# Input projections by seven products of quarters, ahead of the heads, in a two-branch decoder step

## The chip, the cores and the metric

The kernel runs on one core of one Trainium2 chip. The metric is device time in microseconds, from start to end of the program. TensorE (PE) multiplies, VectorE (DVE) and GpSimd (POOL) work on elements, ScalarE (ACT) evaluates functions and copies, and SyncE (SP) issues the transfers. Each engine takes its instructions in its own written order and waits on semaphores of the others.

## The reference

One decoder layer on 560 tokens (16 meta, 512 prompt, 32 sample tokens: 8 batches of 4), width 1024, float32. The core of it:

```python
hn = rmsnorm(x, norm_g)
proj = jnp.einsum('btd,dn->btn', hn, w_in)          # 1024 -> 14344 columns
a_pool, z_pool, q, k, v, o, z_m, i_pre, f_pre, g_pool, g_mlstm = split_projection(proj)
y_pool = multiscale_pool(pool_buf, a_pool, pos0, w_pool, pool_scale) * jax.nn.silu(z_pool)
...
state, h = mlstm_scan(qh, kh, vh, ig, lf, (C, n, m), n_lead)   # 4 heads of 512
h = ((h - mu) * lax.rsqrt(var + EPS)).reshape(B, T, MLSTM_WIDTH) * mh_norm_g
y_mlstm = jax.nn.sigmoid(o) * h * jax.nn.silu(z_m)
u = (jax.nn.sigmoid(g_pool) * (y_pool @ w_branch_pool)
     + jax.nn.sigmoid(g_mlstm) * (y_mlstm @ w_branch_mlstm))
x_out = x + u @ w_out                                # then a last rmsnorm
```

Each head has a 512 x 512 matrix memory C; the kernel returns the new ones for the prompt and for the 8 sample batches, besides the layer's output, the normalisers, stabilisers and pool rows.

## The kernel before, in words

Every float32 operand is held as a sum of two float32r tiles, hi and lo, and every product takes three matmuls: lo hi, hi lo, hi hi (`mm3`, line 129). `weights` (line 113) loads a block of 1024 x 128 weights in one transfer of 512 KB, makes hi on ScalarE (L108) and lo on VectorE (L111). A projection of 128 columns is 8 k blocks x 3 matmuls for each half of the tokens, 48 matmuls of 272 or 280 columns, with the 128 x 128 weights stationary and the normalised tokens `hT_hi`, `hT_lo` moving.

`begin` normalises and transposes the tokens and does the first two blocks of the pool branch; `gates` (line 338) computes everything that has one value per head and token, a chain of small instructions on VectorE. `pooling` projects the pool branch, mixes it, multiplies by its branch weights and stores `up_d`. Then four times `head(h)` (line 580): `unit_v` projects the values with tokens stationary and 512 columns moving (L607, L609); `unit_q`, `unit_k`, `unit_o`, `unit_z` project in blocks of 128; between them stand the head's own products: transposed keys (`k_rows`, L695), the prompt's memory (`prompt_C`, L709), the sample batches' (`sample_C`: read C, L726 and L732, update on VectorE L733, store), scores, key sums, denominators and numerators (L793, L795). The last step of a head, `variances` (line 864), is put into the next head's value projection: a product with ones, the square root on ScalarE (L870), a reciprocal on VectorE (L871), four multiplications. `final` has the merge gates, the mLSTM branch product, the output product and the last norm.

A scheduler with a timing model chooses the order of each engine's instructions among the program's steps; only `Pinned` steps of the beginning keep the written order. Tiles come from rings: `r` (29 tiles of 560 words, queries, keys and other rows), `c` (12 tiles of 1024 words, weights and C) and 8 banks of PSUM. SyncE issues all the large transfers in order.

Of the kernel before, what the change touches and what calls it, by code (L numbers as in the profile page):

```python
# [16 lines left out]
P = 128  # L17
# [14 lines left out]
# token columns: 16 meta, 512 prompt, 32 sample (batch-major)  # L32
# [7 lines left out]
HALF_ALL = ((0, 280), (280, 560))  # L40
HALF_OUT = ((16, 288), (288, 560))


def constants():
# [15 lines left out]
    # rows of the sample queries' part: batches b and b + 4 side by side  # L60
# [8 lines left out]
class Pinned:  # L69
    """An engine whose instructions keep the order they are written in."""  # L70
# [9 lines left out]

class Trunk:
    RS, CS = 29, 12
    G0, Y0 = 1, 3

    def __init__(self, tc, I, O):
        self.tc, self.nc, self.I, self.O = tc, tc.nc, I, O
        self.n = 0
        self.first = []

# [7 lines left out]
    # slabs shared by all phases: [P, 560] and [P, 1024] words  # L97
# [3 lines left out]
    def c(self, name, dt=F32, shape=(D,)):  # L101
        return self.mp.tile([P, *shape], dt, tag="c", name=self.name(name), bufs=self.CS)

    # a float32 tile as the exact sum of two float32r tiles
# [15 lines left out]
    def wcols(self, c0, c=P):  # L120
# [3 lines left out]
    def mm3(self, out, stats, movs):  # L124
        seq = []
        for (sh, sl), (mh, ml) in zip(stats, movs):
            seq += [(sl, mh), (sh, ml), (sh, mh)]
        for j, (s, m) in enumerate(seq):
            self.nc.tensor.matmul(out, s, m, start=(j == 0), stop=(j == len(seq) - 1))  # L129

    def project(self, w, mov, halves, m=P):
        return [self.project_half(w, mov, *t, m) for t in halves]

    def project_half(self, w, mov, t0, t1, m=P):
        hi, lo = w
        ps = self.ps()
        self.mm3(ps[:m, :t1 - t0],
                 [(hi[:, k, :m], lo[:, k, :m]) for k in range(hi.shape[1])],
                 [mov(k, t0, t1) for k in range(hi.shape[1])])
        return ps  # L140

    def hn(self, k, t0, t1):
        return self.hT[0][:, k, t0:t1], self.hT[1][:, k, t0:t1]
# [7 lines left out]
    def run(self):  # L151
        with ExitStack() as ctx:
            tc, nc, I = self.tc, self.nc, self.I
            self.mp = ctx.enter_context(tc.tile_pool(name="main", bufs=1))
            self.psum = ctx.enter_context(tc.tile_pool(name="psum", bufs=8, space=PSUM))
            self.dram = ctx.enter_context(tc.tile_pool(name="scratch", bufs=1, space=DRAM))
            self.w_in = I["w_in"][0].rearrange("(k p) n -> p k n", p=P)
            self.rows_d = self.dram.tile([H, ROWN], F32, name="rows_d")
            self.up_d = self.dram.tile([P, 8, NO], F32, name="up_d")
            self.y_d = self.dram.tile([P, 12, NO], F32, name="y_d")  # L160
            with tc.tile_pool(name="early", bufs=1) as self.ep:
                self.begin()
                self.pooling()
            with tc.tile_pool(name="heads", bufs=1) as self.hp:
                self.heads_begin()
                for h in range(H):
                    self.head(h)
                self.heads_end()
            with tc.tile_pool(name="final", bufs=1) as self.fp:
                self.final()  # L170

# [1 line left out]
    def x_rows(self, t, j):  # L173
        nc, I = self.nc, self.I
        if j == 0:
            nc.sync.dma_start(t[16:], I["x_prompt"][0, 0:112])
            nc.sync.dma_start(t[:16], I["meta_tokens"])
        elif j < 4:
            nc.sync.dma_start(t, I["x_prompt"][0, 128 * j - 16:128 * j + 112])
        else:  # L180
            nc.sync.dma_start(t[:16], I["x_prompt"][0, 496:512])
            nc.sync.dma_start(t[16:48], I["x_sample"].rearrange("b t d -> (b t) d"))

    def begin(self):
        nc, I, mp, ep = self.nc, self.I, self.mp, self.ep
        V, A, G = nc.vector, nc.scalar, nc.gpsimd
        xs = [self.c("x") for _ in range(5)]
        grow = self.c("grow")[:1]
# [8 lines left out]
        wraw = [self.c("wraw", shape=(NK, P)) for _ in range(2)]  # L197
        nc.sync.dma_start(wraw[0], self.wcols(CA))
        self.x_rows(xs[2], 2)
        nc.sync.dma_start(wraw[1], self.wcols(CA + P))  # L200
# [10 lines left out]
        self.hT = [mp.tile([P, NK, NT], F32R, tag="hT", name=n, bufs=2) for n in ("hT_hi", "hT_lo")]  # L211
        self.hS = mp.tile([P, NK, 112], F32R, name="hS")
# [5 lines left out]
        raw = ep.tile([P, NK, 64], F32, name="wg_raw")  # L218
# [3 lines left out]
        seg = ep.tile([H, 2, NT], F32, name="seg")  # L222
# [210 lines left out]
    def pooling(self):  # L433
# [97 lines left out]
        for g in range(1, 4):  # L531
# [3 lines left out]
            if g == 1:  # L535
                self.gate_columns(a)
# [546 lines left out]
```

## Time and profile before

| what | value |
|---|---|
| runs | 1130.87, 1136.81 and 6162.49 us; median 1136.81 |
| profiled execution: span on the core | 1129.6 us (its own time is not listed beside it) |
| mean granted TensorE clock | 0.997 of full speed |
| TensorE, VectorE, ScalarE, GpSimd busy | 1112.0, 613.9, 373.6, 218.8 us |
| matmuls | 7938 |
| transfers | 177.18 MB, mean 157 GB/s |

Busy times count instructions of an engine, overlaps once. A matmul's end is modelled: its duration reads 0.29 us where the next one starts 0.13 us later, so the price of a matmul is read from the spacing of starts in the timeline. In the list of groups a row is one kind of instruction with its count, its busy time and the mean of one in ns, then the idle time of the engine just ahead of it and what ended it.

### The profile page before, as it was taken

How to read it: one execution, taken by the hardware profiler on the slowest of the kernel's cores; microseconds unless marked ns; L12 is line 12 of the kernel's file. 1: busy time of each engine (PE TensorE's matmuls, PEld its weight loads, DVE VectorE, ACT ScalarE, POOL GpSimd, SP SyncE). 2: the span in 40 equal slices, each digit the busy share in tenths (PEclk: the TensorE clock that was granted, in tenths of full speed). 3: DMA queues.
4: the chain of work that ended last, by engine and by line, in shares of the span. 5: the costliest groups of instructions: out<-in, count | busy, mean ns of one | idle time of the engine just before them, and what ended most of it. 6: DMA issues, size and time to landing. Idle time of an engine off the chain costs nothing.

```text
span 1129.6 us, 19419 instructions
## 1 busy us (share of the span) xinstructions
PE 1112.0 (98%) x7938; PEld 1016.7 (90%) x7938; DVE 613.9 (54%) x954; ACT 373.6 (33%) x688; POOL 218.8 (19%) x367
## 2 busy tenths in 40 slices
PE   7999999999999999999999999999999989999997
PEld 6999999989879889979889979889978889999976
DVE  6786732224545755446655456556447465265633
ACT  5642342113222343232342232343222334342322
POOL 4223220003205003205003215003214001020000
PEclk9999999999999999999999999999999999999999
DMA  8432433434566744566654566754565754343512
GB/s 210 128 110 73 111 86 107 126 97 113 178 204 211 231 143 135 176 203 221 222 164 124 173 193 204 232 176 118 167 223 192 237 179 133 107 132 118 180 52 84
DMA packets 188176, 177.18 MB, mean 157 GB/s; under 512 B 12479, under 2 KB 137167, under 8 KB 187563
## 3 DMA queue, kind: packets, MB, share of 16 engines
q1 hardware_dynamic: 188087, 175.94, 50.9%
q8 instruction: 62, 1.02, 0.4%
q14 instruction: 27, 0.22, 0.1%
HBM read 127.80 MB, written 47.39 MB: 155 GB/s over the span
## 4 chain that ended last, share of the span: by engine, by line
PE 77%; DMA 9%; DVE 8%; issue 2%; ACT 1%; SPq 1%; POOL 0%; DVEq 0%; POOLq 0%; ACTq 0%
PE ps L129 57%; PE ps L607 8%; DMA wraw<-in_w_in_dram 6%; DVE C L733 3%; PE ps L709 3%; PE ps L726 2%; PE ps L795 1%; DMA out_dram<-C 1%; PE ps L609 1%; ACT whi L108 1%; DVE wlo L111 1%; DVE vc L767 1%; DMA x<-in_x_prompt_dram 1%; PE ps L695 1%; PE ps L732 1%
## 5 line engine op out<-in xcount | busy, mean ns | idle before, releaser
L129 PE MATMUL ps<-hT_hi,wlo 128*128 128x272 f32 (+1 forms) x1504 | 439.5, 292 | 0.3 <-DVE yp L493 0.3
L129 PE MATMUL ps<-hT_hi,whi 128*128 128x272 f32 (+1 forms) x1504 | 435.3, 289 | 0.0
L129 PE MATMUL ps<-hT_lo,whi 128*128 128x272 f32 (+1 forms) x1504 | 435.1, 289 | 0.0
L111 DVE TENSOR_TENSOR wlo<-wraw,whi 128x1024 fp32r<-128x1024 f32 x134 | 168.0, 1254 | 338.3 <-ACT whi L108 227.0
L129 PEld LDWEIGHTS ps<-hT_hi,wlo 128*128 128x128 f32 x1504 | 284.2, 189 | 15.1 <-issue 10.4
L129 PEld LDWEIGHTS ps<-hT_hi,whi 128*128 128x128 f32 x1504 | 284.7, 189 | 0.0
L129 PEld LDWEIGHTS ps<-hT_lo,whi 128*128 128x128 f32 x1504 | 283.8, 189 | 0.2
L108 ACT CAST whi<-wraw 128x1024 fp32r<-128x1024 f32 x134 | 140.6, 1049 | 393.7 <-DMA wraw<-in_w_in_dram 313.6
L733 DVE SCALAR_TENSOR_TENSOR C<-C,bc,ps 128x512 f32<-128x512 f32 x128 | 87.4, 739 | 6.6 <-PE ps L732 6.6
L129 PE MATMUL ps<-yh,whi 128*128 128x272 f32 x256 | 72.9, 288 | 0.0
L129 PE MATMUL ps<-yl,whi 128*128 128x272 f32 x256 | 72.8, 288 | 0.0
L129 PE MATMUL ps<-yh,wlo 128*128 128x272 f32 x256 | 70.5, 289 | 0.0
L111 POOL TENSOR_TENSOR vl<-v,vh 128x512 fp32r<-128x512 f32 x16 | 31.8, 2023 | 110.3 <-issue 84.5
L607 PE MATMUL ps<-whi,hT_lo 128*128 128x512 f32 x128 | 50.5, 395 | 0.0
L607 PE MATMUL ps<-whi,hT_hi 128*128 128x512 f32 x128 | 50.4, 393 | 0.0
L607 PE MATMUL ps<-wlo,hT_hi 128*128 128x512 f32 x128 | 50.2, 393 | 0.0
L129 PEld LDWEIGHTS ps<-yh,whi 128*128 128x128 f32 x256 | 48.2, 188 | 0.0
L129 PEld LDWEIGHTS ps<-yl,whi 128*128 128x128 f32 x256 | 48.2, 188 | 0.0
L129 PEld LDWEIGHTS ps<-yh,wlo 128*128 128x128 f32 x256 | 46.9, 188 | 0.0
L726 PE MATMUL ps<-C,qm 128*32 128x512 f32 x256 | 40.7, 603 | 0.0
L111 POOL TENSOR_TENSOR kl<-k,kh 128x560 fp32r<-128x560 f32 x16 | 22.3, 1396 | 90.2 <-DVE r_hi L673 77.3
L129 PE MATMUL ps<-ypl,whi 128*128 128x272 f32 x128 | 36.9, 288 | 0.0
(315 smaller groups left out, 1806.7 us busy)
## 6 DMA issues: line engine op xcount, KB each, us to landing
wraw<-in_w_in_dram SPq DMA_DIRECT2D x112, 512.0 KB
C<-in_state_C_dram SPq DMA_DIRECT2D x64, 512.0 KB
out_dram<-C SPq DMA_DIRECT2D x64, 512.0 KB
wraw<-in_w_branch_mlstm_dram SPq DMA_DIRECT2D x16, 512.0 KB
bc<-rows_d SPq DMA_DIRECT2D x4, 1256.0 KB
wraw<-in_w_branch_pool_dram SPq DMA_DIRECT2D x8, 512.0 KB
out_dram<-c SPq DMA_DIRECT2D x16, 256.0 KB
wraw<-in_w_out_dram SPq DMA_DIRECT2D x8, 512.0 KB
```

What stands on the lines that cost most here:

```text
L108: nc.scalar.copy(hi, src)
L111: (lo_on or nc.gpsimd).tensor_tensor(lo, src, hi.bitcast(F32), ALU.subtract)
L129: self.nc.tensor.matmul(out, s, m, start=(j == 0), stop=(j == len(seq) - 1))
L607: nc.tensor.matmul(pv[i], s, w[:, k2], start=(k == 0 and j == 0), stop=(k == 7 and j == 2))
L609: nc.tensor.matmul(pv[4][:112], self.hS[:, k], w[:, k2], start=(k == 0 and j == 0), stop=(k == 7 and j == 1))
L695: nc.tensor.transpose(ps[:, i * P:(i + 1) * P], kw[:, i * P:(i + 1) * P], self.ident)
L709: nc.tensor.matmul(pc, s[:, i], m[:, i], start=(i == 0 and j == 0), stop=False)
L726: nc.tensor.matmul(pqc[r:r + 32], self.qm[:, d, 32 * b:32 * b + 32], Cs[bb // 2][:, bb % 2], start=(d == 0 and g == 0), stop=(d == 3 and g ...
L732: nc.tensor.matmul(pu, kwst[r:r + 12, g], vst[r:r + 12, g], start=True, stop=True, tile_position=(r, 0))
L733: V.scalar_tensor_tensor(C, C, wintb[:, b, 3:4], pu, ALU.mult, ALU.add)
L767: V.scalar_tensor_tensor(t[:n], vh[:n, i].bitcast(F32), vs[:n, i:i + 1], vl[:n, i].bitcast(F32), ALU.subtract, ALU.add)
L795: nc.tensor.matmul(pb[:, o:o + mv.shape[-1] - m], s, mv[:, m:], start=(j == 0), stop=(j == last[True]))
```

## The change

**The product by quarters.** `quad` takes a pair of blocks, 256 columns, at once. The weights are cut into quarters by the two halves of the 1024 inputs and the two blocks of 128 columns; the tokens into quarters by the same halves of the inputs and two halves of 280 tokens (the token columns are laid out anew for this, `COLS`, with `HN` = 280). Seven products of sums of quarters take the place of the eight products of quarters, each of 4 k blocks x 3 matmuls. Four sums of token quarters are made once (`quarter_sums`, on GpSimd, VectorE and ScalarE); four sums of weight quarters are made for each pair on VectorE. Partial results stay in PSUM across products or are kept by ScalarE (`keep`) and added by VectorE (`total`). 47 pairs go this way: q, k, o and z of the heads, z, the merge gates and three of four inputs of the pool branch. The values are projected as before.

**The order.** All projections now stand ahead of the heads, as a list of units. `weave` writes a unit's products side by side with the next unit's weight work, the last but one's late steps, and the steps on the sample's C. Results go to DRAM (`q_d`, `k_d`, `v_d`, `og_d`, `yp_d`, `sg_d`, `qc_d`) and come back in `attention`, where one head's products are woven with the next head's loads and splits. `final` multiplies the pool branch first, with the last head's `variances` in it, then the mLSTM branch, merges and projects.

**Rings.** The 1024-word ring becomes `raw` (4 tiles) and `hl` (14 tiles, seven for each pair); `r` has 12 tiles.

```diff
+def weave(*lists):
+    steps = sorted(((i + 0.5) / len(l), n, i) for n, l in enumerate(lists) for i in range(len(l)))
+    for _, n, i in steps:
+        lists[n][i]()
...
-    def weights(self, src, a, c):
-        raw = self.c("wraw", shape=(a, c))
-        self.nc.sync.dma_start(raw, src)
-        hi, lo = self.c("whi", F32R, (a, c)), self.c("wlo", F32R, (a, c))
-        self.split(hi, lo, raw, self.nc.scalar, self.nc.vector)
-        return hi, lo
...
+    def quad(self, src, lo, dst, scale=None, f21=None, after=(), then=()):
...
+        ahead = [hi1, lambda: hi("w2", "b"), low1, lambda: low("w2", "b"), lambda: add("a", 0, "a", 1),
+                 lambda: add("a", 1, "b", 1), lambda: add("b", 1, "a", 0), lambda: hi("wa", "a"),
+                 lambda: add("b", 0, "b", 1), lambda: hi("wb", "b"), lambda: low("wb", "b"), lambda: low("wa", "a")]
...
+        def p1():
+            product("A", [(w["1"][:, 0, k], w["1"][:, 1, k]) for k in range(4)], quarter(0, 0), True)
+            keep("A", "p1")
+        def p2():
+            product("X", cols("w2", 0), quarter(0, 1), True)
+            total("11", "X", "p1", 1, 1)
+        def p6():
+            product("A", cols("wb", 1), combined("b"), False)
+            keep("A", "u")
+        def p5():
+            product("E", cols("wa", 0), combined("a"), True)
+            keep("E", "e")
+        def p7():
+            product("A", cols("wa", 1), combined("c"), False)
+            total("22", "A", "e", -1, 1)
+        def p3():
+            product("E", cols("w2", 1), combined("d"), False)
+            total("12", "E", "u", 1, -1)
+        def p4():
+            product("A", cols("wb", 0), quarter(1, 1), False)
...
+        for t, u in enumerate(units):
+            if t + 2 < end:
+                for f in units[t + 2].load:
+                    f()
...
+            weave(u.products, units[t + 1].ahead if t + 1 < end else [], old.then + before.after, extra, done)
+            old, before = before, u
...
+        for h, u in enumerate(heads):
+            n = heads[h + 1] if h < 3 else Unit()
+            if h < 3:
+                weave(u.scores, n.ahead1)
+                weave(n.rows, heads[h - 1].late if h else [], n.ahead2[-1:], u.sums)
+            else:
+                weave(u.scores, heads[2].late)
+                weave(u.sums)
+            weave(u.numerators, n.ahead3 if h < 3 else [])
+        self.late = lambda: weave(heads[3].late)
```

Where the change moves instructions, three places matter. First VectorE's queue in the projections of head 0, before, at the first o and z blocks (`sz` is the gate of z, `wlo` the low part of a weight block, `vc` the centred values, C the sample's memory):

```order
L733 SCALAR_TENSOR_TENSOR C_3763<-C_3763,bc_2640,ps_3778 128x512
L836 TENSOR_TENSOR sz_3839<-ps_3789,sz_3839 128x272
L836 TENSOR_TENSOR sz_3839<-ps_3814,sz_3839 128x272
L837 SCALAR_TENSOR_TENSOR og_3603<-og_3603,gmh,sz_3839 128x544
L111 TENSOR_TENSOR wlo_4046<-wraw_4043,whi_4045 128x1024
L767 SCALAR_TENSOR_TENSOR vc_3884<-vh_2643,vs_2645,vl_2644 128x512
```

The same queue now, one pair of weights (`ra`, `rb`) from its first low part to its last, with the totals of the running pair (`zm`) and of the next (`so`) in between:

```order
L212 TENSOR_TENSOR w_252_1706<-ra_1554,w_252_1706 128x512
L253 TENSOR_TENSOR zm_1598<-e_1637,ps_1560 128x272
L205 TENSOR_TENSOR w_256_1724<-rb_1556,w_255_1723 128x1024
L255 TENSOR_TENSOR zm_1598<-ps_1624,u_1620 128x272
L215 TENSOR_TENSOR ra_1554<-ra_1554 128x4x128
L255 TENSOR_TENSOR so_1740<-ps_1727,p_254_1721 128x272
L215 TENSOR_TENSOR ra_1554<-ra_1554,rb_1556 128x4x128
L215 TENSOR_TENSOR rb_1556<-rb_1556,ra_1554 128x4x128
L215 TENSOR_TENSOR rb_1556<-rb_1556 128x4x128
L205 TENSOR_TENSOR wb_1819<-rb_1556,wb_1818 128x1024
L205 TENSOR_TENSOR wa_1783<-ra_1554,wa_1782 128x1024
```

Where one low part for each block stood, each pair now has eight instructions ahead of its products and three totals between them.

Second, VectorE at a head's reciprocal. Before, weights of the next head's values stand around it:

```order
L111 TENSOR_TENSOR wlo_6663<-wraw_6660,whi_6662 128x1024
L868 SCALAR_TENSOR_TENSOR D_742_5593<-D_742_5593,ps_6393 128x240
L869 SCALAR_TENSOR_TENSOR D_742_5593<-D_742_5593,ps_6394 128x304
L871 RECIPROCAL D_742_5593<-D_742_5593 128x544
L873 TENSOR_TENSOR og_5448<-og_5448,D_742_5593 128x544
```

Now the low parts of the next head's transposed keys (`kwr`) stand behind it:

```order
L1418 SCALAR_TENSOR_TENSOR D_1625_9814<-D_1625_9814,ps_10196 128x240
L1419 SCALAR_TENSOR_TENSOR D_1625_9814<-D_1625_9814,ps_10197 128x304
L1282 SCALAR_TENSOR_TENSOR kw_10157,npr<-k_1698_10155,wsb_8798 128x528
L1289 TENSOR_TENSOR st_2_8775<-kw_10131,st_2_8775 128x16
L1446 RECIPROCAL D_1625_9814<-D_1625_9814 128x544
L1289 TENSOR_TENSOR st_3_8777<-kw_10157,st_3_8777 128x16
L140 TENSOR_TENSOR kwr_10191<-ps_10184,kwr_10191 128x512
```

and TensorE at the same place has the variances (`sl`, `sh` with ones), five transposes, and then the product that reads `kwr_10191`:

```order
L1353 MATMUL ps_10196<-sl_10043,ones 128x240
L1355 MATMUL ps_10197<-sl_10043,ones 128x304
L1353 MATMUL ps_10196<-sh_10042,ones 128x240
L1355 MATMUL ps_10197<-sh_10042,ones 128x304
L1299 MATMUL ps_10211<-ident,kw_10100 128x128 x4
L1300 MATMUL ps_10212<-ident,st_1_8773 96x128
L1312 MATMUL ps_10228<-vr_10081,kwr_10191 128x512 x3
```

What moved: before, TensorE went on from the variances to value projections, which read no result of VectorE's chain.

Third, VectorE in the beginning, at the end of the gates' chain (`gnQ`, `rw`, `ws`, `em`) and the last low part of the first head's value weights (`wlo_627`):

```order
L608 TENSOR_SCALAR rw_73_596<-rw_73_596,gb_531 4x144
L615 TENSOR_SCALAR ws_597<-ga_532,rw_73_596 4x128
L926 TENSOR_TENSOR wlo_627<-wraw_402,whi_626 128x1024
L608 TENSOR_SCALAR rw_72_595<-rw_73_596,gb_531 4x272
L615 TENSOR_SCALAR ws_597<-ga_532,rw_73_596 4x128
L212 TENSOR_TENSOR w_95_769<-ra_761,w_95_769 128x512
```

The value projection of head 0, which stood behind the pool branch, now stands first, and its last weights come behind most of the chain.

## Rows read from the trace of the kernel before

**Rows 1.** The page, part 1: busy time of each engine, share, instructions.
```profile
PE 1112.0 (98%) x7938; PEld 1016.7 (90%) x7938; DVE 613.9 (54%) x954; ACT 373.6 (33%) x688; POOL 218.8 (19%) x367
```
**Rows 2.** The page, part 4: the chain that ended last, by engine.
```profile
PE 77%; DMA 9%; DVE 8%; issue 2%; ACT 1%; SPq 1%; POOL 0%; DVEq 0%; POOLq 0%; ACTq 0%
```
**Rows 3.** Waits of TensorE: us in total, times, longest.
```profile
PE ps L77 <- DVE xn L77: 2.9, 4, 1.6
PE ps L942 <- DVE og L857: 2.7, 1, 2.7
```
**Rows 4.** Timeline of TensorE, 272 columns: start, us, engine, line, operation.
```profile
99.74 0.29 PE L129 MATMUL ps<-hT_hi,whi 128*128 128x272 f32 x1
...
101.76 0.29 PE L129 MATMUL ps<-hT_hi,wlo 128*128 128x272 f32 x1
```
**Rows 5.** Timeline of TensorE, 280 columns.
```profile
299.76 0.29 PE L129 MATMUL ps<-hT_hi,whi 128*128 128x280 f32 x1
...
302.06 0.29 PE L129 MATMUL ps<-hT_hi,whi 128*128 128x280 f32 x1
```
**Rows 6.** Views of two tiles: count, then shortest, median and longest in ns.
```profile
L111 DVE TENSOR_TENSOR wlo<-wraw,whi x134: 1204/1226/2401, 26.3 to 1041.0; 128x1024 fp32r<-128x1024 f32 x134
...
L767 DVE SCALAR_TENSOR_TENSOR vc<-vh,vs,vl x20: 736/744/1801, 354.8 to 903.4; 128x512 f32<-128x512 f32 x16, 48x512 f32<-48x512 f32 x4
```
**Rows 7.** Groups of VectorE by form: count, busy us, mean ns, idle before.
```profile
L111 DVE TENSOR_TENSOR wlo<-wraw,whi 128x1024 fp32r<-128x1024 f32 x134 | 168.0, 1254 | 338.3 <-ACT whi L108 227.0 <-PE ps L129 67.3 <-PE ps L609 42.5
L733 DVE SCALAR_TENSOR_TENSOR C<-C,bc,ps 128x512 f32<-128x512 f32 x128 | 87.4, 739 | 6.6 <-PE ps L732 6.6
L767 DVE SCALAR_TENSOR_TENSOR vc<-vh,vs,vl 128x512 f32<-128x512 f32 x16 | 15.1, 1006 | 0.0
L871 DVE RECIPROCAL D<-D 128x544 f32<-128x544 f32 x4 | 14.2, 3554 | 3.4 <-ACT D L870 3.4
...
L836 DVE TENSOR_TENSOR sz<-ps,sz 128x272 f32<-128x272 f32 x32 | 14.0, 437 | 15.0 <-ACT sz L835 15.0
...
L837 DVE SCALAR_TENSOR_TENSOR og<-og,gmh,sz 128x544 f32<-128x544 f32 x16 | 12.5, 783 | 0.4
...
L111 DVE TENSOR_TENSOR kwl<-ps,kwh 128x512 fp32r<-128x512 f32 x16 | 10.9, 681 | 0.0
```
**Rows 8.** Groups of ScalarE by form.
```profile
L108 ACT CAST whi<-wraw 128x1024 fp32r<-128x1024 f32 x134 | 140.6, 1049 | 393.7 <-DMA wraw<-in_w_in_dram 313.6 <-DMA wraw<-in_w_branch_mlstm_dram 31.0 <-DMA wraw<-in_w_branch_pool_dram 22.1
...
L835 ACT ACTIVATE sz<-ps 128x272 f32<-128x272 f32 x32 | 12.5, 392 | 10.4 <-PE ps L129 10.4
...
L870 ACT ACT_TABLE_LOAD x4 | 5.1, 1283 | 0.1
...
L870 ACT ACTIVATE D<-D 128x544 f32<-128x544 f32 x4 | 2.6, 659 | 6.2 <-DVE D L869 6.2
```
**Rows 9.** Groups of GpSimd by form: its longest low parts.
```profile
L111 POOL TENSOR_TENSOR vl<-v,vh 128x512 fp32r<-128x512 f32 x16 | 31.8, 2023 | 110.3 <-issue 84.5 <-DVE vh L110 25.8
```
**Rows 10.** Timeline of VectorE: the gates' chain, near its start and end.
```profile
45.51 0.73 DVE L359 SCALAR_TENSOR_TENSOR az<-zf 4x560 f32<-4x560 f32 x1
...
62.55 0.43 DVE L385 TENSOR_SCALAR gnQ<-gQ 4x560 f32<-4x560 f32 x1
```
**Rows 11.** Windows: stretch, length, busy time of five engines, granted clock, DMA share, GB/s.
```profile
370.00:400.00 30.00, 29.84 (x230) 26.36 (x228) 19.50 (x28) 10.29 (x21) 0.00 (x0) 1.00 0.80 259
...
924.70:928.00 3.30, 3.30 (x17) 3.30 (x16) 3.27 (x8) 0.66 (x3) 0.00 (x0) 0.50 0.53 207
```
**Rows 12.** Timeline of TensorE at the heads' end: gaps in brackets, then slow matmuls.
```profile
916.47 0.29 PE L795 MATMUL ps<-Ph,vl 80*128 80x48 f32 x1 [1.08 <-DVE vl L111]
...
923.70 0.61 PE L942 MATMUL ps<-ident,nnew 128*32 128x128 f32 x4 [2.66 <-DVE og L857]
...
924.80 0.43 PE L129 MATMUL ps<-hT_hi,whi 128*128 128x272 f32 x1
...
927.98 0.35 PE L129 MATMUL ps<-hT_lo,whi 128*128 128x272 f32 x1
```

More of the change, by code (lines that the diff above doesn't have):

```diff
@@ L142, in hn, with project @@
-    def hn(self, k, t0, t1):
-        return self.hT[0][:, k, t0:t1], self.hT[1][:, k, t0:t1]
+            self.nc.tensor.matmul(out, s, m, start=(first and j == 0), stop=(j == len(seq) - 1),
+                                  skip_group_check=not check)
+    def project(self, st, mov, halves):
+        out = []
+        for t0, t1 in halves:
+            ps = self.ps()
+            self.mm3(ps[:, :t1 - t0], st, [mov(k, t0, t1) for k in range(len(st))])
+            out.append(ps)
+        return out
@@ new lines, in projections_begin @@
+    def projections_begin(self):
+        self.tl = self.ip.tile([P, 8, 48], F32, name="tl")
+        self.pooled, self.zs = {}, {}
+        self.vst, self.sw, self.kwst, self.pqc, self.vend = {}, {}, {}, {}, {}
+        v = self.unit_v(0)
+        a = self.unit_a(0, self.first)
+        for u in v:
+            for f in u.load:
+                f()
+        gates = self.gates()
+        other = [lambda: next(gates, None)] * 32
+        sums = self.quarter_sums()
+        for f in a.products + v[0].ahead:
+            f()
+        for n, u in enumerate(v):
+            k = 4 - n
+            first = [sums[:len(sums) // k], other[:len(other) // k]]
+            sums, other = sums[len(first[0]):], other[len(first[1]):]
+            weave(u.products, v[n + 1].ahead if n < 3 else [], *first)
+        for _ in gates:
+            pass
+        return v[3], a
@@ new lines, in sums, with unit_z, tiles, gate @@
+            return [tails] + [lambda lev=lev: level(lev) for lev in range(g + 1)] + [mean]
+        after = sums(0) + sums(1)
+        if first:
+            return Unit([], [], [begin, lambda: whole(0), lambda: whole(1), lambda: rows(0), lambda: rows(1)], after)
+        u = self.quad(self.wcols(CA + g * 256), 0, dst, after=after)
+        u.products[:1] = [begin, u.products[0]]
+        u.products += [lambda: rows(0), lambda: rows(1)]
+        return u
+    def unit_z(self, g):
+        V, A = self.nc.vector, self.nc.scalar
+        z = []
+        def tiles():
+            z.extend(self.r("zx") for _ in range(2))
+            return z
+        def gate(n):
+            s = self.r("zs")
+            A.activation(s[:, :NO], z[n][:, :NO], AF.Sigmoid)
+            V.tensor_tensor(z[n][:, :NO], z[n][:, :NO], s[:, :NO], ALU.mult)
+            self.zs[2 * g + n] = z[n]
+        return self.quad_out(self.wcols(CZP + g * 256), tiles, after=[lambda: gate(0), lambda: gate(1)])
@@ L765, in centre_v @@
[L765 to L784 removed]
+        room = []
@@ L953, in final @@
+        u.sums = [*each(weight, 0, 1, 2, 3, 4), key_sums]
+        u.numerators = [load_og, denominators, *each(numerator, 0, 1, 2, 3)]
+        u.late = [variances, lambda: V.reciprocal(D2, D2), *each(scaled, 0, 1, 2, 3)]
+        return u
     def final(self):
@@ new lines, in final @@
+        yp = both("yp", self.yp, 2)
+        for k in range(8):
+            y_in(yp, k, self.yp_d[:, k])
+        up = []
+        for g in range(4):
+            for d, pb in branch(wp, [yp], g):
+                t = row("up")
+                nc.sync.dma_start(t, self.sg_d[:, d])
+                for q in range(2):
+                    sl = slice(272 * q, 272 * q + 272)
+                    V.tensor_tensor(t[:, sl], pb[q][:, :272], t[:, sl], ALU.mult)
+                up.append(t)
+            if g == 0:
+                self.late()
```

1377 lines of the change are left out of this document (824 added, 553 removed).

## The prediction

> **What bounds it now.** I read the busy shares first: TensorE is busy 1112.0 of 1129.6 us, VectorE 613.9, ScalarE 373.6 [rows 1]. Then the chain of waits: 77% of it is TensorE [rows 2]; the reader should see that neither weights nor splits set the pace. Then TensorE's own waits: the two largest are 2.9 us at the beginning and one of 2.7 at the heads' end [rows 3], so there is almost nothing to win but in the number of matmuls. A time can fall only if TensorE gets fewer, and it stays only if TensorE goes on finding its operands ready.
>
> The runs are 1130.87 and 1136.81 us, beside one of 6162.49, so the median 1136.81 is 0.6% above the profiled span of 1129.6. My sum goes against the span; I add 2.5 us, between the 1.3 and 7.2 by which those runs lie above it. Borders for faster and slower by 2% are 1114.1 and 1159.5.
>
> **What is removed.** Modelled ends overlap, so I price a matmul by start spacing: 16 intervals from 99.74 to 101.76 us give 0.126 us for 272 columns, I take 0.125 [rows 4]; 18 intervals from 299.76 to 302.06 give 0.128 for 280 [rows 5]. A 256-column pair goes from 96 matmuls to 84 (seven products, four k, three matmuls). 36 pairs of 272 columns and 11 of 280 (eight k pairs, three pool inputs): 432 x 0.125 + 132 x 0.128 = **-70.9**. The stretch is pure TensorE, so all of this is on the path while operands are ready. 16 more transposes (rows of the last keys, now apart) at no more than 0.126: **+2.0**. The 2.66 us gap at the heads' end, with 1.4 of slow matmuls behind it (below), goes, since the pool branch now stands there: **-4.1**. Sum so far 1056.6.
>
> **What is added beside it: VectorE.** A pair cost it two low parts of 1.226 [rows 6]. Now, ahead of the products, one low part and four additions of 512 elements (0.681 each, the nearest row), three low parts of 1024 (1.226): 7.08; then three totals at 0.437: 1.31 [rows 7]. So 8.4 us beside 84 x 0.125 = 10.5 on TensorE. ScalarE gets 3.5 casts of 1.049 and four copies of 0.392, 5.2 us [rows 8]: half of TensorE's, so I cost it at nothing; the cover is gone only if it doubles. But VectorE works in order, one unit ahead at most, as the ring of fourteen tiles holds two pairs, and its totals wait for TensorE. So what counts is each unit, not the sum. With the gate of an mLSTM z pair (two multiplications of 0.783 and two of about the same) VectorE has 11.5 against 10.5; a step on the sample's memory adds 4 x 0.739 = 2.96 [rows 7], and less to TensorE; the four mixes are the narrow places: 24 matmuls, 3.0 us, while VectorE has their four totals, the next pair's 7.08 and mostly a gate: 9 to 15 us. With these prices for each of the 63 units, the sum of the larger of the two engines' times is 56 above TensorE's alone, 34 of it at the mixes (6, 9, 9, 10). Lower bound 0 if TensorE's first two products of the next pair, which need only the first low parts, bridge the rest. That bridge is 3 us at each excess, so I take **+20**; ends 0 and 56.
>
> [...] Low parts mostly take 1.226 us, but up to 2.401; the centred values 0.744, but up to 1.801 [rows 6]. [...]
>
> **Begin.** The gate rows are a serial chain on VectorE, from 45.51 to 62.55 us already [rows 10]. It now shares VectorE with eight quarter sums and eight low parts ahead of the first pair, and the order puts the last v weights' low part behind the chain; TensorE, without the pool products that covered it, gets there some 5 us earlier. Ends 0 and 8, I take **+6**, near the upper end because the order shows the low part behind.
>
> **From projections to heads.** Values, keys and queries come back from DRAM, then weighted keys, transposes and low parts on GpSimd precede the first product. No row shows it; between 0 (loads started early) and 11 us (some 3 for a transfer, a product with weights and its transposes, four low parts of up to 2.023 [rows 9]). I take **+8**.
>
> **Heads.** Before, scores, denominators and variances had projections beside them. Now only other heads' products are there. At heads 1 and 2 the order puts variances, then five transposes, then a product of the next head that needs a low part behind the reciprocal: two additions of about 0.437, square root 0.659 with its table 1.283 [rows 8], reciprocal 3.554, low part 0.681 [rows 7], together 7.1, less about 1 of transposes: 6 us, twice. [...] So 12 + 3, and 5 for the last head, which has no next head beside its key sums and low parts on GpSimd (a few subtractions of 1 to 2 us each): **+20**. [...] Transfers: some 9 MB a head take 35 us at the 259 GB/s that went with a share of 0.80 [rows 11]; a head's own products are some 64,000 columns, 30 us at 0.126 for 272 and more where they are narrow. [...]
>
> **Sum.** 1056.6 + 20 + 6 + 8 + 20 = 1110.6; with 2.5 for the run, **1113 us**.
>
> **Rivals.**
> 1. *The cover holds nearly everywhere.* Bridges between units and other heads' products take most of the four losses; at most 15 us remain: 1056.6 + 2.5 + 13 = 1072. For it: in a plain pair VectorE has a fifth left, ScalarE half. Against: in-order queues and four mixes. Chance 0.23.
> 2. *VectorE sets the pace of the projections* (the slower side). Place: every z pair, state step and mix. The instructions need only be longer than the rows: at 1.05 times, the sum of unit maxima gives 68 instead of 56, and 1056.6 + 68 + 34 + 2.5 = 1161, beyond the border; from there it decides, if no bridge holds. At 1.1 times it is 86: 1179 us. For it: totals wait in VectorE's queue ahead of additions; centred values average 1.35 times their undisturbed time. [...] Chance 0.14.
> 3. *The clock falls over and over.* If each of 47 pairs ended in a gap like the 2.66 us one, the clock alone would lose 47 x 1.4 = 66, the gaps themselves 20 as above: 1179. The trace bears it out by one gap; the matmul behind one of 1.08 still took 0.29 us against 0.43 [rows 12], and the gaps expected at plain pairs are shorter. [...] Chance 0.05.
> That the pairs still use eight products is ruled out: the order counts 84 matmuls for each.
>
> **Numbers.** Forecast 0.58, of which about half falls below 1114; rival 1 all faster: faster 0.48. Forecast's other half and the low part of rival 2: same 0.35. Rivals 2 and 3 above 1159.5: slower 0.17. The range goes from near the sum without losses to the upper border: 1066 to 1160.
>
> **What would show it.** Right: 84 matmuls in 10.5 us in plain pairs; TensorE gaps of 3 to 6 us behind mixes, with VectorE busy throughout; gaps of about 6 us at two reciprocals with a lower clock behind them; TensorE's busy time near 1045. Wrong: gaps inside ordinary pairs (rival 2); a granted clock under 0.97 over the projections (rival 3); TensorE waiting for transfers in the heads, which I priced at nothing; or none of the gaps (rival 1).

## The result: 9% slower, and the profile after

The changed kernel takes 1237.95 us (median of 4 runs, 1231.44 to 1245.15) against 1136.42 for the kernel before in the same session (median of 4, one of them an outlier of 6162.49); the ratio, taken without that run, is 1.092, with a 95% interval of 1.087 to 1.097. The prediction said 1113 with a range up to 1160, so the result lies outside on the slow side. The profiled span is 1234.6 us against 1129.6. The page of the changed kernel, parts 1, 2 and 4 (busy us, share and count; tenths in 40 slices; the chain by engine), answering to [rows 1, 2]:

```profile
PE 1120.4 (91%) x7390; PEld 977.1 (79%) x7390; DVE 840.4 (68%) x1319; ACT 531.5 (43%) x1003; POOL 218.8 (18%) x350
...
PE   6869999999999999999999999846966777999997
...
PEclk9879999999999999999999999967987878999999
...
PE 73%; DMA 9%; DVE 8%; ACT 4%; issue 2%; SPq 2%; POOL 2%; POOLq 0%; DVEq 0%; ACTq 0%
```

TensorE has 548 instructions fewer and is busy 8 us longer. From the fourth slice to the 25th its row is full, and yet that stretch is longer than it should be. Two stretches have holes and a lower clock: the first three slices, and the heads (slices 27 to 34). TensorE's waits, answering to [rows 3] (total us, times, longest):

```profile
PE ps L1312 <- DVE kwr L140: 31.1, 4, 11.1
PE ps L1299 <- DVE kw L1282: 15.0, 2, 8.8
PE ps L1353 <- DVE sl L140: 8.6, 2, 7.3
PE ps L166 <- ACT yp L137: 7.7, 1, 7.7
PE ps L1353 <- POOL dl L140: 6.6, 1, 6.6
PE ps L940 <- DVE wlo L926: 5.9, 1, 5.9
...
PE ps L166 <- ACT p L238: 3.0, 1, 3.0
...
PE ps L166 <- ACT u L238: 2.0, 1, 2.0
...
PE ps L1053 <- POOL kst L1041: 1.4, 2, 1.2
...
PE ps L937 <- DVE wlo L926: 1.1, 1, 1.1
```

The last four are all the waits between 100 and 798 us, 7.5 us. The windows, as in [rows 11], for the projections, the heads and one bad piece of the beginning:

```profile
100.00:798.00 698.00, 690.49 (x4732) 588.69 (x4732) 533.62 (x848) 313.54 (x559) 51.77 (x138) 1.00 0.63 206
...
798.00:1040.00 242.00, 166.41 (x972) 148.25 (x971) 151.57 (x213) 118.64 (x266) 117.43 (x148) 0.81 0.57 191
...
28.00:38.00 10.00, 7.54 (x29) 7.17 (x29) 1.84 (x4) 1.91 (x8) 7.26 (x9) 0.51 0.83 261
```

The granted clock was 1.00 over the projections, 0.81 over the heads (0.50 from 858 to 863 us, 1.00 from 870 to 875), and 0.51 behind the early gaps.

**An account by stages.** Busy time hides the projections' loss, because matmuls overlap in it (0.29 us each where they start 0.125 apart). So I price each matmul of a form at its median start spacing, the four-in-a-row groups at what they take together, and call the rest of a stage its loss. By that count TensorE's work fell from 1090.5 to 1027.5 us, and the losses rose from 39 to 207:

| stage | loss before | loss after | more | what the prediction had |
|---|---|---|---|---|
| beginning (to 60; now to 100 us) | 11.5 | 38.2 | 26.7 | 6 |
| projections (to 924 with the heads between; now to 798) | 18.4 | 63.9 | 45.5 | 20 |
| from projections to heads, and heads (now to 1040) | in the row above | 96.8 | 96.8 | 28 |
| last stage | 9.6 | 7.6 | -2.0 | -4.1 |

63 less work and 167 more loss make +104, and the spans differ by 105. The single rows depend on the prices: with other medians for the same forms a row moves by up to 4 us. Of the forecast -4.1, the 2.66 us gap lay before 924 us, so it is counted in the row of the projections; now TensorE has one of 8.0 us between the heads and the last stage (1018 to 1026 us, the wait for `yp` above), counted in the row of the heads.

**Where the 45 us of the projections are.** Pairs run as forecast; starts 0.125 apart, as in [rows 4]. What is dear stands between them. TensorE's timeline at two steps on the sample's memory (start, us, line; L1081 is C times q, two records for each product, L1090 the update of C):

```profile
165.07 0.29 PE L166 MATMUL ps<-hT_hi,w 128*128 128x272 f32 x1
165.29 1.02 PE L1081 MATMUL ps<-C,qm 128*8 128x512 f32 x2
166.25 0.39 PE L166 MATMUL ps<-hT_hi,w 128*128 128x272 f32 x1
166.48 0.29 PE L166 MATMUL ps<-hT_lo,w 128*128 128x272 f32 x1
...
167.95 1.04 PE L1081 MATMUL ps<-C,qm 128*8 128x512 f32 x8
...
240.33 0.49 PE L1090 MATMUL ps<-vst,kwst 12*128 12x512 f32 x1
240.75 0.50 PE L937 MATMUL ps<-whi,hT_hi 128*128 128x512 f32 x1
```

and the same update in the kernel before:

```profile
306.27 0.51 PE L732 MATMUL ps<-vst,kwst 12*128 12x512 f32 x4
306.71 0.66 PE L695 MATMUL ps<-ident,kw 128*128 128x128 f32 x4
```

One product alone (165.29 to 166.25) holds TensorE for 0.96 us; four side by side (x8) take 0.97 on average. One update alone takes 0.42, four together 0.44. The kernel gives the four products the positions (0, 0) to (0, 96) by `tile_position` and the four updates (0, 0) to (96, 0); the times show that they run side by side, but only while they stand next to each other. The matmul before such a group starts 0.22 us ahead of it, and the one behind it 0.23 us ahead of the next matmul, instead of 0.125, so some 0.1 us more go on either side; what takes them was not shown. The scheduler now set other matmuls between the members of a group: the 32 groups of four products came out as 58 pieces, the 32 groups of updates as 62. The sums of start spacings: products 38.5 us before, 60.0 now; updates 13.9 and 27.6; what the neighbours lost 6.6 and 17.1. Together they grew by (60.0 - 38.5) + (27.6 - 13.9) + (17.1 - 6.6) = 45.7 us, which is the stage's 45.5 as closely as such a count can tell.

**Where the heads' 97 us are.** Twelve gaps of 1.5 to 11.4 us by the start spacings, 77 together (21.6 of them before the first product of weights and values), and 19 us beside them, nearly all in matmuls that ran while the granted clock was low (0.50 over 858 to 863, 906 to 911 and 1026 to 1031 us). Four of the gaps (brackets: idle us and releaser):

```profile
858.85 4.63 PE L1312 MATMUL ps<-vr,kwr 128*128 128x512 f32 x10 [11.14 <-DVE kwr L140]
...
906.50 2.07 PE L1312 MATMUL ps<-vr,kwr 128*128 128x512 f32 x4 [7.30 <-DVE kwr L140]
...
955.34 4.93 PE L1312 MATMUL ps<-vr,kwr 128*128 128x512 f32 x12 [7.19 <-DVE kwr L140]
...
987.89 0.54 PE L1353 MATMUL ps<-sl,ones 128*128 128x240 f32 x1 [7.30 <-DVE sl L140]
```

The second and third are the two reciprocals that the prediction named. In the first, VectorE's queue shows why:

```profile
851.88 4.85 DVE L1282 SCALAR_TENSOR_TENSOR kw<-k,wsb 128x528 f32<-128x528 f32 x1 [1.19 <-POOL Pl L140]
...
893.81 0.69 DVE L1282 SCALAR_TENSOR_TENSOR kw<-k,wsb 128x528 f32<-128x528 f32 x1
```

The same instruction takes 0.69 us elsewhere. Beside the long one GpSimd was subtracting, by its own timeline:

```profile
852.02 2.47 POOL L140 TENSOR_TENSOR vr<-v,vr 128x512 fp32r<-128x512 f32 x2
854.46 0.48 POOL L1369 TENSOR_TENSOR D<-D,bc 128x144 f32<-128x144 f32 x1
854.90 1.25 POOL L140 TENSOR_TENSOR vr<-v,vr 128x512 fp32r<-128x512 f32 x1
```

### The profile page after: what moved, and what is told of

Its sections match the earlier page's. It is cut to its first block, busy times and chain, and to the rows that moved or that the text cites. A ratio compares the mean times of both kernels' runs of the same rounds, so it can differ in the third digit from the quotient of the medians.

```text
span 1234.6 us, 19611 instructions
## 1 busy us (share of the span) xinstructions
PE 1120.4 (91%) x7390; PEld 977.1 (79%) x7390; DVE 840.4 (68%) x1319; ACT 531.5 (43%) x1003; POOL 218.8 (18%) x350
## 4 chain that ended last, share of the span: by engine, by line
PE 73%; DMA 9%; DVE 8%; ACT 4%; issue 2%; SPq 2%; POOL 2%; POOLq 0%; DVEq 0%; ACTq 0%
PE ps L166 52%; PE ps L937 5%; PE ps L1081 5%; PE ps L1312 4%; PE ps L1090 2%; DMA rb<-in_w_in_dram 2%; DMA x<-in_x_prompt_dram 1%; PE ps L1355 1%; DVE sqn L1409 1%; PE ps L940 1%; DMA v<-v_d 1%; DVE kw L1282 1%; DMA bc<-rows_d 1%; DMA ra<-in_w_in_dram 1%; DMA k<-k_d 1%
## 5 line engine op out<-in xcount | busy, mean ns | idle before, releaser
L166 PE MATMUL ps<-hT_hi,w 128*128 128x272 f32 (+1 forms) x752 | 161.4, 296 | 0.0
L166 PEld LDWEIGHTS ps<-hT_hi,w 128*128 128x128 f32 x752 | 125.0, 191 | 18.5 <-issue 6.5
L1095 DVE SCALAR_TENSOR_TENSOR C<-C,sw,ps 128x512 f32<-128x512 f32 x128 | 90.0, 743 | 36.8 <-PE ps L1090 36.5
L166 PE MATMUL ps<-hT_lo,w 128*128 128x272 f32 (+1 forms) x376 | 109.7, 292 | 0.0
L1312 PE MATMUL ps<-vr,kwr 128*128 128x512 f32 x192 | 56.2, 448 | 31.1 <-DVE kwr L140 31.1
L166 PE MATMUL ps<-Sb_hi,wb 128*128 128x272 f32 (+1 forms) x376 | 81.1, 293 | 3.0 <-ACT p L238 3.0
L166 PE MATMUL ps<-Sc_hi,wa 128*128 128x272 f32 (+1 forms) x376 | 80.7, 293 | 2.0 <-ACT u L238 2.0
L166 PE MATMUL ps<-Sa_hi,wa 128*128 128x272 f32 (+1 forms) x376 | 80.8, 291 | 0.0
L166 PE MATMUL ps<-hT_hi,wb 128*128 128x272 f32 (+1 forms) x376 | 79.5, 291 | 0.0
L166 PE MATMUL ps<-Sd_hi,w 128*128 128x272 f32 (+1 forms) x376 | 79.4, 290 | 0.0
L166 PEld LDWEIGHTS ps<-Sc_hi,wa 128*128 128x128 f32 x376 | 62.1, 188 | 13.9 <-issue 6.5
L166 PEld LDWEIGHTS ps<-hT_lo,w 128*128 128x128 f32 x376 | 71.9, 191 | 0.0
L1081 PE MATMUL ps<-C,qm 128*8 128x512 f32 x256 | 64.1, 594 | 0.0
```

The costliest lines, as they stand in the source:

```text
L166: self.nc.tensor.matmul(out, s, m, start=(first and j == 0), stop=(j == len(seq) - 1), skip_group_check=not check)
L1081: nc.tensor.matmul(self.pqc[h][r:r + 8], self.qm[h % 2][:, d, b], Cs[bb // 2][:, bb % 2], start=(d == 0 and g == 0), stop=(d == 3 and g == 1),
L1095: V.scalar_tensor_tensor(C, C, self.bview(self.sw[h][:, 0])[:, 4 * g + bb, 3:4], pu, ALU.mult, ALU.add)
L1312: nc.tensor.matmul(pc, w[:, s, i], vr[i][:, m], start=(i == 0 and j == 0), stop=False)
```

## Experiments

The first theory: the pairs' saving is real and the projections are bound by TensorE; the split memory groups took it away there, and the heads lost the rest because nothing covers their chains. The rival for the projections was VectorE as the bound, as the prediction had it.

**Eight products instead of seven.** If TensorE is the bound, going back to eight must cost what seven save.

```diff
-        return Unit([load], ahead, [p1, p2, p6, p5, p7, p3, p4], after, then)
+        return Unit([load], ahead, [f for half, col in ((0, 0), (1, 0), (0, 1), (1, 1)) for f in two(half, col)],
+                    after, then)
```

> The changed kernel with its pairs as eight products of quarters again, 96 matmuls: two casts and two low parts ahead, no sums of weight quarters (the token sums are still made and not read). Theory A (TensorE bounds the projections, so the seven products do bring their share): 60 to 75 us more, 1295 to 1310. Theory B (VectorE set the pace, and it now has 5.9 us less a pair): 0 to 30 us more, 1235 to 1265.

1302.25 us (one run), span 1300.4: +66, although VectorE's busy time falls from 840.4 to 651.7. Of the 66, 50 lie between the first and the last matmul of the pairs (760 us instead of 710) and 10 in the heads, which the scheduler ordered anew. So VectorE didn't set the pace, and the saving is there. The 564 added matmuls are 71 us by [rows 4, 5]; the order, which changes too, gives some of it back (products in 42 pieces, 40.7 us instead of 60.0; updates in 78, 33.2 instead of 27.6), and TensorE's 7.5 us of waits are gone.

**No work on the sample's memory.** All updates of C and all but a few of its products are left out, and with them part of the output.

```diff
...
-        return [products, lambda: update(0), lambda: update(1)]
+        return [products] if j == 7 else []
```

> The changed kernel without the sample memory's matmuls and updates (the last step of a head alone keeps its four query products); loads and stores of the memory stay, its values are not computed. Theory A (TensorE pays for the scattered small matmuls, 88 us of starts and about 35 of switches): the span falls by 105 to 125 us, to 1110 to 1130. Theory B (they cost TensorE what they cost before, 52 us, and VectorE's 95 us go as well): by 55 to 90 us, to 1145 to 1180, with gaps of TensorE at the mixes and gated pairs as the rest.

1154.68 us (one run), span 1152.8: -82, and -88 in the projections (from the first matmul of the pairs at 88.2 to the last at 798.2 in the changed kernel, 93.9 to 715.5 here). The amount is near 45.7 for splitting and some 45 for the grouped work. But it is less than the 105 that I had written for the first theory and inside the 55 to 90 of the second; and as VectorE loses 128 updates of 0.743 as well, this run doesn't tell the two apart. The run above does.

**TensorE's order in the projections as written.** All of TensorE's instructions there keep the order of the program.

```diff
+        self.pe = Pinned(self.tc, self.nc.tensor)
...
-            self.nc.tensor.matmul(out, s, m, start=(first and j == 0), stop=(j == len(seq) - 1),
+            self.pe.matmul(out, s, m, start=(first and j == 0), stop=(j == len(seq) - 1),
```

> The changed kernel with TensorE's instructions of the projections in the written order, so that a step's four query products stand together, while its updates stay two and two. Theory A (scattered small matmuls cost TensorE): query products 60 to about 33 us of starts, updates as before near 28, without the 12.8 us of waits for the memory's totals that the version with four updates together showed; the last pair starts at 775 to 785 us instead of 798. Rival: the rigid order costs as much as it gains, 795 to 805.

1231.35 us (one run), span 1229.6. Products in 32 pieces: 31.2 us instead of 60.0, as the theory has it. The updates, written as two and two, are 64 pieces and 39.9 us, some 12 of them waits that I hadn't expected. The last matmul of the pairs starts at 785.6 instead of 798.2; the heads (from their first transposed keys to the pool branch) take 225 instead of 219, in another order of the scheduler's.

**The same with the four updates of a step together.**

```diff
-            for bb in (2 * j2, 2 * j2 + 1):
+            for bb in range(4):
...
-        return [products, lambda: update(0), lambda: update(1)]
+        return [products, lambda: update(0)]
```

> The changed kernel, with TensorE's instructions of the projections kept in the written order, and a step's four updates of the sample's memory written together instead of two and two. Theory A (the step's small matmuls, which run four side by side when they stand together, were split into ones and twos by the order): the memory's two groups fall from 60 and 28 us of TensorE starts to about 35 and 14, and some 10 to 20 us of switches beside them go too; 1234.6 us of span becomes 1175 to 1195. Theory B (VectorE sets the pace of the projections, so TensorE's order does not matter, and a rigid order adds stalls): 1225 to 1260.

1227.04 us, ratio to the kernel before 1.081 (1.076 to 1.085). The projections end 17.4 us earlier, at 780.7, but less than the 45 comes back, and the span, 1232.2, lies in the range of the second theory. Products took 32.7 us instead of 60.0, but updates, in 32 pieces, 37.0 instead of 27.6: with a fixed order TensorE waits where the scheduler had let it go on. The heads, again in another order, got 13 us longer. From TensorE's waits in this kernel, the first in the heads, the second in the projections:

```profile
PE ps L1303 <- DVE bc L1328: 15.7, 3, 7.6
PE ps L80 <- DVE C L1098: 12.8, 17, 3.0
```

**Splitting alone, in the kernel before.** The last two runs mix the cure with new waits. So the reverse: the kernel before, whose waits are small, with six matmuls of 128 columns added to each of the 32 steps (results unused). They stand ahead of the four products (joined), or in the middle of products and updates (twos), or between all of them (ones). `spare(n)` adds n of them, and in all three kernels products, updates and added matmuls keep the written order; the twos have the first pair of lines, the ones the second pair, in the loops over a step's products and its updates:

```diff
+                spare(3 * int(bb == 1))
...
+                    spare(3 * int(bb == 2))
```

```diff
+                spare(int(apart and bb < 3))
...
+                    spare(int(apart))
```

> The kernel before, with 192 added matmuls of 128 columns (six at each of the 32 steps on a sample's memory, results thrown away), all six ahead of the step's four C products; the four products and the four updates stay side by side. Control for the two runs beside it. Theory A (memory products and updates run four side by side, and a group costs nearly the same time whether it holds one or four) and its rival (that they are split costs nothing; the projections lost their 45 us by waits) both expect the 192 x 0.06 = 12 us of the added matmuls, and perhaps some at the switches: 1142 to 1152 us.

> The same 192 matmuls, but three stand in the middle of the four C products and three in the middle of the four updates, so that these run in twos, about as split as the changed kernel has them (58 and 62 bursts), in a kernel whose waits are otherwise those of before. Theory A: C products 64 bursts at 0.96 = 61 instead of 38.5, updates 64 at 0.43 = 27.5 instead of 13.9, and 64 more switches at 0.1 to 0.2 = 6 to 13: 42 to 49 above the run with the same matmuls put ahead, near 1190 us. Rival: within 10 of it.

> The same 192 matmuls, one after each of the first three C products and of the first three updates: all in ones. Theory A: C products 128 bursts at 0.96 = 123 instead of 38.5, updates 128 at 0.43 = 55 instead of 13.9, 192 more switches at 0.1 to 0.2 = 19 to 38: 145 to 163 above the run with the matmuls put ahead, 1290 to 1310 us. Rival: within 20 of it.

Joined 1162.04 us, twos 1192.04, ones 1321.97 (ratios to the kernel before 1.023, 1.051 and 1.167, with intervals of 1.019 to 1.027, 1.049 to 1.054 and 1.163 to 1.172). TensorE's timeline of the joined kernel at its first step (L734 is C times q, L743 the update, L729 an added matmul):

```profile
306.73 1.06 PE L734 MATMUL ps<-C,qm 128*32 128x512 f32 x8
307.73 0.50 PE L743 MATMUL ps<-vst,kwst 12*128 12x512 f32 x4
```

The same step of the kernel with twos:

```profile
306.84 1.05 PE L734 MATMUL ps<-C,qm 128*32 128x512 f32 x4
307.83 0.55 PE L729 MATMUL ps<-kwst 128*128 128x128 f32 x3
308.31 1.05 PE L734 MATMUL ps<-C,qm 128*32 128x512 f32 x4
309.29 0.50 PE L743 MATMUL ps<-vst,kwst 12*128 12x512 f32 x2
```

And of the kernel with ones, products first, updates behind:

```profile
306.36 1.04 PE L734 MATMUL ps<-C,qm 128*32 128x512 f32 x2
307.33 0.33 PE L729 MATMUL ps<-kwst 128*128 128x128 f32 x1
307.59 1.04 PE L734 MATMUL ps<-C,qm 128*32 128x512 f32 x2
...
311.03 0.49 PE L743 MATMUL ps<-vst,kwst 12*128 12x512 f32 x1
311.45 0.33 PE L729 MATMUL ps<-kwst 128*128 128x128 f32 x1
```

Start spacings of all products: 31.9, 62.9 and 124.9 us; of all updates: 13.9, 27.3 and 55.1. Twice the pieces, twice the time, whatever a piece holds. That is the theory's slope: 160 us from joined to ones, where 145 to 163 were expected; the rival had allowed 20. In themselves joined and ones came out above what was written, by 10 and 12 us. From joined to twos the median rose by 30, not 42 to 49, as the joined run was itself dearer than I wrote: its added matmuls took 23.1 us and not 12, it waited 9.0 us for low parts of the values at the denominators, and its clock was 0.987 against 0.998. Over the steps themselves the twos cost 55 us more (129.4 against 74.4, with the matmul ahead of each). So splitting as such, with hardly a wait of TensorE's in the twos and the ones, costs about what the projections lost.

**Cover in the heads.** 448 more matmuls of 272 columns (112 for each head; the text below says 400), 56 us of work with unused results, are put ahead of the products that wait.

```diff
...
+            if d == 0:
+                self.spare(48)
...
+        self.spare(24)
...
+        self.spare(40)
```

> The changed kernel with 400 extra matmuls of 272 columns in the heads, on constants, into a bank that nothing reads: 48 before each head's first prompt memory, 24 before its denominators, 40 before its variances, kept at these places; at full clock 56 us of TensorE if they are starting the moment that they may, less where the listing shows fewer. Theory E (TensorE waits there for results that do not depend on it, and its clock falls for want of work): the time stays within 12 us of the changed kernel, or falls by up to 15 because the clock stays up. Rival F (TensorE's own work is the length of the heads): 40 to 56 us more.

1247.12 us, ratio 1.099 (1.096 to 1.102), +9 on the changed kernel. Heads and last stage take 431.5 us instead of 420.7: 56 us of work for 11. The heads alone, with 408 of the added matmuls, take 220.4 instead of 219.1. The granted clock over 798 to 1040 rose from 0.81 to 0.92, as this kernel's window shows,

```profile
798.00:1040.00 242.00, 205.41 (x1369) 190.38 (x1368) 138.97 (x209) 118.58 (x265) 123.86 (x150) 0.92 0.58 189
```

and the group of waits that was the largest, 31.1 us before the edit, is now this one:

```profile
PE ps L1323 <- DVE kwr L140: 3.8, 1, 3.8
```

So the chains run on while TensorE works, and 51 us of work in the heads fill its gaps or come back by the higher clock; in the kernel before, projections stood there.

**The heads' low parts on VectorE instead of GpSimd.** One of four such lines (values, keys, score weights and key sums):

```diff
...
-            kT.append(self.parts(k32s.pop(d), lambda s: key("k" + s), G))
+            kT.append(self.parts(k32s.pop(d), lambda s: key("k" + s), V))
```

> The changed kernel with the low parts of the heads (values, keys, score weights, key sums) on VectorE instead of GpSimd. Theory C (GpSimd's long subtractions stand in the heads' chains and hold up VectorE): TensorE's waits in front of the prompt memory fall from 31 us to under 20, the last head's wait of 6.6 us to about 5, and the half clock behind them shortens; 15 to 30 us less, 1205 to 1220. Theory D (loads, reciprocal and the lack of other TensorE work make the waits): within 6 us of 1234.6.

1228.97 us, ratio 1.084 (1.081 to 1.087): -9, where 15 to 30 were expected. The heads take 210.3 us instead of 219.2. The long instructions are gone: the squares (`sqn`) had 705, 1122 and 4860 ns as shortest, median and longest before the edit, and now, in the view of that tile,

```profile
L1409 DVE TENSOR_TENSOR sqn<-sqn,sqn x12: 712/715/718, 880.2 to 1008.2; 128x544 f32<-128x544 f32 x12
```

with the weighted keys' longest at 1.26 us instead of 4.85. So GpSimd's work was their cause, but VectorE now does that work itself: TensorE's waits for `kwr` fall from 31.1 to 19.9 us, those for `sl` rise from 8.6 to 17.0.

**The beginning.** The gates' weight copy is put behind the token parts on ScalarE, and the values' low parts ahead of the gates' chain.

```diff
-        self.split(wg[:, :, 0:64], wg[:, :, 64:128], raw, A, G)
+        pA.copy(wg[:, :, 0:64], raw)
...
-        for f in a.products + v[0].ahead:
+        for f in a.products + [f for u in v for f in u.ahead]:
...
-            weave(u.products, v[n + 1].ahead if n < 3 else [], *first)
+            weave(u.products, *first)
```

> The changed kernel with two moves in the beginning: ScalarE's copy of the gate weights stays behind the tokens' last parts, and the low parts of the first head's four value weights are written ahead of the gates' chain. Theory G (the chain and a copy that waits for a transfer stand in front of what TensorE needs): the waits of 5.9 us on the value weights and of 2.5 us on the tokens go, and the clock falls less; first pair and end 8 to 18 us earlier, 1215 to 1227. Rival: the chain, later now, is waited for elsewhere, within 4 us of 1234.6.

1245.68 us, ratio 1.098 (1.095 to 1.101), no gain. The first pair starts at 80.6 instead of 88.2, and the 5.9 us wait for `wlo` is gone; at the third pair 1.2 us of the lead are left, at the sixth 0.1, and a new wait of 3.6 us for one of VectorE's totals stands between. The pairs end at the same time as before the edit (797.9 against 798.2), and the rest of the difference is the heads, 227 us instead of 219 in an order that the scheduler chose anew. So the two waits alone were not what held the beginning. It fits this that VectorE's work, which must be done before the pairs can run, sets its length, but no run shows it.

**The reciprocal out of the way.** A head's variances and reciprocal go behind the next head's keys.

```diff
-                weave(n.rows, heads[h - 1].late if h else [], n.ahead2[-1:], u.sums)
+                weave(n.rows, n.ahead2[-1:], u.sums)
...
-            weave(u.numerators, n.ahead3 if h < 3 else [])
+            weave(u.numerators, n.ahead3 if h < 3 else [], heads[h - 1].late if 0 < h < 3 else [])
```

> The changed kernel with a head's variances, root, reciprocal and scaling moved behind the next head's transposed keys, into its numerators. Theory H (the reciprocal in VectorE's queue makes the waits in front of the prompt memory of heads 2 and 3): those two waits fall from 7.3 us to 3 or less, 6 to 14 us less in all with the clock, 1220 to 1229. Theory I (those waits come from loads and from GpSimd's low parts of the values, the reciprocal only hides behind them): within 4 us of 1234.6.

1245.99 us, ratio 1.099 (1.096 to 1.101). The two gaps fell from 7.6 to 3.6 and to 5.0, less far than to the 3 expected, and the time lies outside the ranges of both theories, because two other waits took their place among TensorE's:

```profile
PE ps L1353 <- DVE sl L140: 14.4, 1, 14.4
PE ps L166 <- ACT st L1288: 10.4, 1, 10.4
```

The 8 us by which this median lies above the changed kernel's are not clear of chance: the two intervals overlap, and four versions above that left the heads' code alone (eight products, both fixed orders, the beginning) had heads of 225 to 232 us instead of 219, by the scheduler's order alone. The 210 with the low parts on VectorE lie below all of these.

No version of the changed kernel that computes everything came near the kernel before. Seven products inside the old structure, where projections cover the heads, were not tried; the sums of the tokens' quarters would have to stay in SBUF during the heads, and whether there is room for them was not shown.

## Why the prediction was wrong

1. **Removed matmuls (-70.9, +2.0): right.** Undoing them costs 50 us in their stretch, and there the order gives back 14 and the waits 7.5; the pairs' spacing is that of [rows 4, 5]. The third term beside them, -4.1 for the gap at the heads' end, was wrong (its 1.4 is what the trace before shows behind that gap: 14 spacings of 0.227 instead of 0.125, at a granted clock of 0.50 [rows 11, 12]): in its place stands one of 8.0, because SP issues the load of the pool branch's rows only at 1021.68 us (the last line of the timeline in 5).
2. **VectorE beside the pairs (+20; rival 2): wrong in its mechanism.** The stage lost 45.5, but its waits are 7.5 us in all. Low parts stayed at a mean of 1.221 to 1.226 us against 1.254 in [rows 7], and VectorE was busy 534 of 698 us. The bridge that I trusted with two thirds of the excess held nearly all of it: in the order that the scheduler made, TensorE hardly waits. That the loss lies between my ends of 0 and 56 is therefore luck. The price of that order lay elsewhere (3).
3. **The step that failed here: "a step on the sample's memory adds 2.96, and less to TensorE".** I priced a moved step on VectorE and left its TensorE part at what it took in the kernel before. With its neighbours it took 1.8 us of TensorE there (38.5, 13.9 and 6.6 over 32 steps) and 3.3 now (60.0, 27.6 and 17.1), more than VectorE's 2.96. Its price depends on what stands beside it. The timeline before shows four updates in 0.44 us, above; the order of the changed kernel shows products in twos and updates alone between other matmuls. I read that order at three places, and at none of these.
4. **Beginning (+6): too small by 21.** The foretold wait for the low part behind the gates' chain came, 5.9 us. Missed were the token cast behind a ScalarE copy that waits for its transfer (2.46 us), two more waits of 2.2 and 2.6, and the lower clock behind the gaps (0.51 over 28 to 38 us). Taking away the wait of 5.9 and the ScalarE copy moved the loss to later waits, so what makes this stage long stays open.
5. **From projections to heads (+8): 21.6.** Three gaps stand in a row (8.8, 6.2 and 5.5 us of waiting), each for a result of the one chain that I had priced once. The loads of keys and decay rows are issued behind the last stores, at 801 to 804 us, as SP's timeline shows:

```profile
799.40 0.88 SPq L869 DMA_DIRECT2D sg_d<-sg  x2
...
801.32 0.42 SPq L1434 DMA_DIRECT2D wsb<-rows_d  x1
...
803.85 0.61 SPq L1279 DMA_DIRECT2D k<-k_d  x1
808.91 3.89 SPq L1429 DMA_DIRECT2D bc<-in_c_sel_dram  x2
...
1021.68 0.97 SPq L1463 DMA_DIRECT2D y<-yp_d  x2
```

   Behind the keys at 803.85 SP waits for the decay rows before it issues the next keys, at 813.79.
6. **Heads (+20): 75. The second step that failed, and the larger one: "Now only other heads' products are there", and then a price for three waits alone.** The waits that I named were of the right size: 6 each at the reciprocals against gaps of 7.6, 5 at the last head against 6.8. But I counted three, and there were nine (56 us), two more of them in and behind the last head (7.6 and the 8.0 of point 1). I costed the clock at 3 us, twice the 1.4 of point 1; no run shows that 3, and in its place most of the other 19 us is the clock's. With the cover gone, every chain of the stage shows, not only those that I could point to.
7. **VectorE beside GpSimd.** Nothing in the +20 stands for it. The weighted keys took 4.85 us instead of 0.69 beside GpSimd's subtractions; moving that work gave 9 us. The 4.85 us are longer than any one of the four GpSimd instructions beside them (at most 1.25), so a wait for a single one doesn't explain them; what does was not shown.
8. **Rivals.** The cover didn't hold (1), VectorE didn't set the pace (2), and the clock didn't fall at pairs (3): 1.00 over the projections. What came was a slow case that I hadn't written: a stage of short chains left without cover, beside small matmuls torn apart.

What stays open: how much of the heads' other 70 us a better order could win. The two edits that aimed at single chains there moved waits to the next chain; one won 9 us, the other nothing that is clear of the scheduler's other choices. The order of SP's loads at their beginning and at their end wasn't tried.

## What to carry to other kernels

When a change moves small matmuls that run side by side, count in the new order how many of them still stand next to each other; their price here was per piece (0.96 us for one product, 0.97 for four), not per matmul, and a busy row of 9s does not show it. When work is taken from one stage and put into another, ask what covered the waits of the stage that it left: price every chain there as if it stood bare, and add the lower clock behind each gap (here 0.50 over the 5 us behind one of 11.1). A wait that is removed from such a stage mostly turns up at the next chain, so look at the end of the stage and not at the wait.

## What the runs showed of the hardware

- Four products of 128x512 f32 take 0.97 us side by side with 8 columns of weights and 1.00 with 32, and one alone takes 0.96 and 0.98; four updates on 12 rows each take 0.43 to 0.44, and one alone 0.42. Tearing 32 such steps wholly apart, with a matmul of 128 columns in each place between, cost 160 us against the same matmuls ahead of the steps.
- A VectorE instruction of 0.69 us took 4.85 beside a row of GpSimd subtractions, and another of 0.71 took 4.86; with the heads' low parts moved to VectorE none of the squares, the second kind, took over 0.72.
- Gaps of 1.5 to 11.4 us, twelve in 240 us, left a mean granted clock of 0.81, and 408 unused matmuls of 272 columns put into them raised it to 0.92.
